# A mixer-and-experts block: second gate's weights behind the first expert's, routing on the residual's sums, first-layer weights laid out by partitions

## The chip, the cores and the metric

The kernel runs on one core of one Trainium2 chip. The metric is the device time of one execution in microseconds (us); the median of three runs is compared. All data are float32 in HBM, about 450 MB of it weights that are read once.

## What is computed

One block on 256 tokens of width 1024. A condition row `c` makes six modulation rows; a mixer (attention with forget gates, gated linear attention, pooling) works on the modulated x; the first layer norm follows; then 32 experts, 4 per token, and the second layer norm.

```python
cond = silu(c)
shift1, scale1, gate1, shift2, scale2, gate2 = split(cond @ w_ada + b_ada, 6)
h = x * (1 + scale1) + shift1
z = h @ w_in + b_in                      # 1024 -> 2582: heads, gates, pool inputs
y = concat([o_fox, o_gla, o_pool]) @ w_out
x = layer_norm(2**0.25 * x + (1 + gate1) * y, ln1_g, ln1_b)
h = x * (1 + scale2) + shift2
logits = h @ w_router + b_router         # 32 experts
gate = softmax(top_k(logits, 4))
y = sum over a token's 4 experts of gate * (clamped_swiglu(h @ w_gate_up[e] + b) @ w_down[e] + b)
x = layer_norm(2**0.25 * x + (1 + gate2) * y, ln2_g, ln2_b)
```

## The kernel before

**Loads.** All large weights pass through ring tiles of 2 MB (16 KB in each of 128 partitions), and SyncE issues their loads in the order of the program text. Each load waits until the slot that it gets is free, and the next one waits behind it. Ahead of the experts the ring has 5 slots (`NA`). In order they hold the first modulation's weights (`ada`) and the input projection's (`wz`), alternating; two small groups of constants; the rest of the input projection; the second modulation's shift and scale (`adam`); the output projection (`wo`); and the two gates' weights, `ada_g1` and `ada_g2` (`adag`, two tiles each). Then come the experts: four tiles of `w_gate_up` (`g`), with two tiles of `w_down` (`d`) of the expert before behind them. A second ring of 3 slots (`NB`, `ring2`) is opened for the experts; it lies on memory that the first layer's tiles (`early`) leave. Of every eight expert tiles, the first five go to the first ring and the last three to the second. The sum of the two is how far loads run ahead of TensorE.

**Layout.** `w_ada`, `w_in` and `w_out` are read from HBM as they are, with k rows by partitions: for `ada`, each piece read in one go is 128 columns (512 B) in the first tile and 256 columns (1 KB) in the others; for `wz`, 1520 and 272 columns; for the other tiles, 1024 or some 400.

**First layer.** `tokens_to_columns` transposes x on TensorE (4 transposes for each of four groups) and copies it to `hT`. `modulate` makes shift and scale of a pair of columns and applies them to `hT` in place. The k loop then multiplies `hT[:, k]` with the 1792 columns of `wz1[k]`: 6 products (`pqk`) and 8 (`pz`); a float32 product shows as two instructions in the trace. Attention, linear attention and pool follow and fill `oT`, the left operand of the output projection (`py`, 64 instructions; L134 is the line of the helper `mm` that issues nearly all products).

**Gates.** `ada_g1` and `ada_g2` are each summed on VectorE over k with weights `cond` (one multiply and seven multiply-adds, each over 1024 columns), to `acc` and `g2p`. Both stand in front of the output projection in the text. `last_scale` completes `g2p` behind expert 0's gate-up products, and `down` of each expert multiplies with it.

**Routing**, for each half t of the tokens: residual `y` in two column halves with `bn_stats`; norm to `n1`; 8 transposes of `n1`; scale `hA` and shift `hB` on the way out of PSUM to `h2T`; the router product in four groups of 32 rows, re-summed by a second product; top 4; positions `posm`. When both halves are done, `dispatch` of the first pair of experts makes one-hot rows `pp`, gathers `xg` from `n1` by products (`pxg`, 16 instructions for each half of the tokens), and scales it by `hA`, `hB`.

**Experts.** For each expert, `gate_up` (64 instructions and the bias), the clamp, the transposes, and one expert later `down`. Pairs share a dispatch. In front of expert 12 (`PAIR_MORE` = 6 pairs) all loads up to eight tiles ahead are issued, and then a branch on the largest expert's count is taken (`more_slots`; not entered with these inputs).

## Time and profile before

| | us |
|---|---|
| median of 3 runs | 1128.66 |
| lowest and highest | 1127.93, 1134.68 |
| profiled execution | 1129.8 |
| its span, first to last instruction | 1128.0 |
| TensorE matmul busy | 1035.4 (92%) |
| VectorE busy | 318.7 (28%) |
| ScalarE busy | 98.8 (9%) |
| mean DMA rate | 398 GB/s |

Matmul ends are modelled, so a busy TensorE is not one at its peak. The granted clock is given as a share of 2.4 GHz; 0.50 is 1.2 GHz. A queue's instruction (SPq) spans the time in which the listed issues were made, waits included.

### The profile page before, as it was taken

The page shows a single profiled execution, that of the slowest core. Times are in us where ns is not written, and L with a number is a line of the kernel's source. Part 1 is how long each engine was busy: PE and PEld are TensorE (multiplying, and loading weights), DVE is VectorE, ACT ScalarE, POOL GpSimd, SP SyncE. Part 2 cuts the span into 40 slices and gives each one's busy share as a digit, 9 for nine tenths or more (in the row PEclk, how much of TensorE's full clock was granted, in tenths as well). Part 3 has the DMA queues.
Part 4 walks back from the last instruction along what each step waited for, and adds up shares of the span by engine and source line. Part 5 has one row for each costly group of instructions (what it writes and reads, how often), then busy time and mean ns, then how long its engine had stood idle before and what let it go on. Part 6 is the DMA issues. An engine that isn't in the chain of part 4 may idle for free.

```text
span 1128.0 us, 11046 instructions
## 1 busy us (share of the span) xinstructions
PE 1035.4 (92%) x4734; PEld 436.9 (39%) x4735; DVE 318.7 (28%) x587; ACT 98.8 (9%) x205; POOL 41.5 (4%) x43
## 2 busy tenths in 40 slices
PE   6999998999999999996999999989989898989795
PEld 3656545434333333333344343423333333333231
DVE  1459694322222122211122221213221121211113
ACT  1024112100000000000000000000000000000100
POOL 2270000000000000000000000000000000000000
PEclk9999897999999999998999999999999999999998
DMA  9997499999999999999899999999999999999992
GB/s 324 348 385 283 181 378 373 428 423 428 428 428 427 428 428 428 428 427 423 344 427 428 428 428 426 428 427 428 428 428 427 428 429 427 428 427 428 428 414 92
DMA packets 52998, 449.49 MB, mean 398 GB/s; under 512 B 5056, under 2 KB 18768, under 8 KB 28496
## 3 DMA queue, kind: packets, MB, share of 16 engines
q1 hardware_dynamic: 52320, 447.90, 95.7%
q8 instruction: 39, 0.64, 0.2%
q10 hardware_dynamic: 624, 0.83, 0.2%
q14 instruction: 15, 0.12, 0.0%
HBM read 447.67 MB, written 1.05 MB: 398 GB/s over the span
## 4 chain that ended last, share of the span: by engine, by line
PE 29%; DMA 22%; DVE 1%; issue 1%; ACT 0%; POOL 0%; DVEq 0%; POOLq 0%
DMA d<-in_w_down 22%; PE gu L134 13%; PE py L134 7%; PE pxg L134 4%; PE ya L134 3%; PE pyl L134 1%; PE paT L837 1%; DVE yb L855 0%; DVE aT L839 0%; DVE res L919 0%; ACT n L931 0%; PE pln L134 0%; DVE r L1038 0%; DVE yl L1015 0%; DVE st L1019 0%
## 5 line engine op out<-in xcount | busy, mean ns | idle before, releaser
L134 PE MATMUL gu<-g,xg 128*64 128x512 f32 x2048 | 462.5, 595 | 14.0 <-DMA g<-in_w_gate_up 12.6
L134 PEld LDWEIGHTS gu<-g,xg 128*64 128x64 f32 x2048 | 143.2, 137 | 295.5 <-issue 261.0
L134 PE MATMUL py<-d,aT 128*64 128x512 f32 x992 | 227.1, 600 | 13.8 <-DMA d<-in_w_down 12.5
L825 DVE TENSOR_SCALAR g<-gu 128x512 f32<-128x512 f32 x32 | 22.1, 692 | 410.1 <-PE gu L134 410.1
L134 PEld LDWEIGHTS py<-d,aT 128*64 128x64 f32 x992 | 70.0, 137 | 150.5 <-issue 140.8
L134 PE MATMUL pxg<-pp,n 128*128 128x128 f32 x512 | 77.0, 302 | 14.9 <-DVE aT L839 7.0
L134 PEld LDWEIGHTS pxg<-pp,n 128*128 128x128 f32 x512 | 69.2, 208 | 43.0 <-issue 29.6
L855 DVE TENSOR_TENSOR yb<-py,g2p 64x512 f32<-64x512 f32 x60 | 41.3, 689 | 139.0 <-PE py L134 138.4
L134 PE MATMUL ya<-yb,sg_None 128*128 128x512 f32 x120 | 58.2, 607 | 4.9 <-DVE yb L855 4.8
L829 ACT ACTIVATE s<-g 128x512 f32<-128x512 f32 x32 | 20.2, 630 | 464.4 <-DVE g L825 464.4
L793 DVE TENSOR_SCALAR xg<-pxg,hA,hB 128x128 f32<-128x128 f32 x64 | 25.8, 409 | 99.2 <-PE pxg L134 90.0
L791 ACT ACTIVATE xg<-pxg,hB,hA 128x128 f32<-128x128 f32 x64 | 28.7, 457 | 274.3 <-DVE xg L793 273.6
L134 PE MATMUL pz<-wz,hT 128*128 128x512 f32 (+2 forms) x128 | 52.4, 547 | 0.0
L169 POOL TENSOR_TENSOR rsb<-rtb,half 128x2 f32<-128x2 f32 x1 | 0.7, 701 | 950.9 <-DVE rtb L168 950.9
L839 DVE COPY aT<-paT 128x512 f32<-128x512 f32 x32 | 22.1, 692 | 43.9 <-PE paT L837 43.8
L134 PE MATMUL py<-wo,oT 128*128 128x512 f32 x64 | 30.9, 629 | 0.2 <-ACT oT L642 0.2
L134 PEld LDWEIGHTS ya<-yb,sg_None 128*128 128x128 f32 x120 | 20.4, 189 | 26.9 <-issue 17.4
L134 PEld LDWEIGHTS pz<-wz,hT 128*128 128x128 f32 x128 | 23.4, 190 | 17.3 <-issue 14.3
L837 PEld LDWEIGHTS paT<-kc,l 128*128 128x128 f32 x128 | 18.0, 209 | 25.3 <-DVE l L831 15.4
L837 PE MATMUL paT<-kc,l 128*128 128x128 f32 x128 | 23.7, 308 | 0.0
L831 DVE TENSOR_TENSOR l<-l,s 128x512 f32<-128x512 f32 x32 | 22.1, 691 | 3.4 <-DVE l L830 0.5
L134 PE MATMUL pqk<-hT,wz 128*128 128x256 f32 x96 | 22.2, 381 | 0.7 <-DVE hT L332 0.7
(245 smaller groups left out, 519.1 us busy)
## 6 DMA issues: line engine op xcount, KB each, us to landing
g<-in_w_gate_up SPq DMA_DIRECT2D x128, 2048.0 KB, 30.4
d<-in_w_down SPq DMA_DIRECT2D x62, 2048.0 KB, 30.4
adam<-in_w_ada SPq DMA_DIRECT2D x4, 2048.0 KB, 16.7
adag<-in_w_ada SPq DMA_DIRECT2D x4, 2048.0 KB, 9.0
ada<-in_w_ada SPq DMA_DIRECT2D x6, 1024.0 KB, 11.1
wz<-in_w_in SPq DMA_DIRECT2D x8, 760.0 KB, 9.5
wo<-in_w_out SPq DMA_DIRECT2D x2, 1536.0 KB, 10.0
ada<-in_w_ada SPq DMA_DIRECT2D x4, 512.0 KB, 7.4
```

The source lines that it names most:

```text
L134: T.matmul(o, l, r, start=start, stop=stop, skip_group_check=True, **kw)
L169: G.tensor_tensor(o, t[:, :n], half[:, :n], op=OP.pow)
L791: A.activation(xg[:, k], bs[k // 4][:, k % 4], AF.Identity, bias=hB[:, k:k + 1], scale=hA[:, k:k + 1])
L793: V.tensor_scalar(xg[:, k], bs[k // 4][:, k % 4], hA[:, k:k + 1], hB[:, k:k + 1], op0=OP.mult, op1=OP.add)
L825: V.tensor_scalar(g, gu[:, 0], LIMIT, None, op0=OP.min)
L829: A.activation(s, g, AF.Sigmoid, scale=SW_ALPHA)
L831: V.tensor_mul(l, l, s)
L837: T.transpose(b[:, j], act[:, j::4], ident)
L839: V.tensor_copy(aT, b)
L855: V.tensor_mul(yb[m * CAP:(m + 1) * CAP, n * 512:(n + 1) * 512], b[r], g2p[r, n * 512:(n + 1) * 512])
```

## The change

- `w_ada`, `w_in` and `w_out` are laid out ahead of the kernel so that each ring tile is one contiguous run per partition (7 to 16 KB); each of `ada`, `wz` and `wo` is loaded by one DMA where it had two.
- x is given a second time, transposed (`xT`), and loaded straight into `hT`; `tokens_to_columns` goes. x itself is loaded behind `wo`.
- The first gate's weights are loaded ahead of `wo`, and summed ahead of the linear attention's output part; the router's weights are loaded earlier.
- The second gate's weights are loaded as two more tiles behind expert 0's four gate-up tiles, and summed behind expert 0's gate-up products; `last_scale` moves behind expert 1's. The place of the three second-ring tiles in each eight changes from the last three to the fourth to sixth.
- Routing: the router's weights are multiplied by `hA` and `hB` once (`wr2`, and their column sums `rrow`). The residual `y` is transposed as it is, before the norm; the logits are (product with `wr2`) times the norm's scale plus a row. The first pair's one-hot rows and gather are made for each half inside the loop, to `xgA`.
- Some tiles share memory to make room for `xgA` (`o_gla` with `z_gr`, the bias rows with `oT`, and others).

```diff
-            i = int(turn[0] % (NA + NB) >= NA)
+            i = int(3 <= turn[0] % (NA + NB) < 3 + NB)
...
+    def summed(acc, ts):
+        A.mul(acc, ts[0], cond[:, 0:1])
+        for k in range(1, KT):
+            V.scalar_tensor_tensor(acc, ts[k], cond[:, k:k + 1], acc, op0=OP.mult, op1=OP.add)
+    def load_columns(j, i, name):
+        t = ring_tile(name)
+        o = (4 + 2 * (3, 4, 2, 5).index(j) + i) * 4096
+        SY.dma_start(t, w_ada[:, o:o + 4096])
+        return [t[:, k * D:(k + 1) * D] for k in range(4)]
...
-            t = t.rearrange("p (k s n) -> p k s n", k=KT, s=2)
-            for h in range(2):
-                SY.dma_start(t[:, :, h], w_ada[0, :, h * D + cc * 256:h * D + (cc + 1) * 256]
-                             .rearrange("(k p) n -> p k n", p=P))
+            SY.dma_start(t, w_ada[:, cc * 4096:(cc + 1) * 4096])
...
-            SY.dma_start(t[:, 0:W1], w_in[0, k * P:(k + 1) * P, 0:W1])
-            SY.dma_start(t[:, W1:], w_in[0, k * P:(k + 1) * P, C_GA:])
+            SY.dma_start(wz1[-1][:, k % 2], w_in[:, k * WZ:(k + 1) * WZ])
...
-        SY.dma_start(xs[:, :, 0:256], xv[:, :, 0:256])
+        SY.dma_start(hT[:, 0:2], xTv[:, 0:2])
         load_z1(0)
-        SY.dma_start(xs[:, :, 256:], xv[:, :, 256:])
         first_ada[1]()
+        SY.dma_start(hT[:, 2:], xTv[:, 2:])
...
+        ada_g1 = load_cols(2, "adag1")
         wo = {}
...
-        ada_g1 = load_cols(2, "adag1")
-        ada_g2 = load_cols(5, "adag2")
+        SY.dma_start(xs, x[0].rearrange("(t p) d -> p t d", p=P))
...
-        tokens_to_columns(0, "z")
         modulate(0, 1)
...
+        acc1 = la_.tile([P, D], F32, tag="acc", name="acc1")
+        summed(acc1, ada_g1)
+        o_gla = la_.tile([P, TT, GVW], F32, tag="gr", name="o_gla")
...
+        for j, h in enumerate((hA, hB)):
+            V.tensor_mul(wr2[:, j], wr, h[:, :, None].to_broadcast([P, KT, NE]))
+        V.tensor_reduce(wrs, wr2.rearrange("p j k e -> p j e k"), axis=AX.X, op=OP.add)
+        mm(b[:, 0:2 * NE], ones, wrs.rearrange("p j e -> p (j e)"), True, False)
+        mm(b[:, NE:2 * NE], colv[:, 80:81].to_broadcast([P, P]), kc[:, K_I4:K_I4 + NE], False, True)
+        V.tensor_copy(rrow, b[:, 0:2 * NE].rearrange("p (j e) -> p j e", j=2))
...
                 V.bn_stats(st6[:, n], y)
+                b = bank(f"ph{t}{n}").rearrange("p (j s) -> p j s", j=4)
+                for j in range(4):
+                    T.transpose(b[:, j], twos(xs[:, t], 4 * n + j), ident)
+                A.copy(h2T[:, 4 * n:4 * n + 4, t * P:(t + 1) * P], b)
...
+            V.scalar_tensor_tensor(row, rrow[:, 0], nmr, rrow[:, 1], op0=OP.mult, op1=OP.add)
+            b = bank(f"plg{t}")
+            for k in range(KT):
+                mm(b[:, 0:NE], h2T[:, k, t * P:(t + 1) * P], wr2[:, 0, k], k == 0, k == KT - 1)
+            V.scalar_tensor_tensor(lg[:, t], b[:, 0:NE], rs, row, op0=OP.mult, op1=OP.add)
...
-            for k in range(KT):
-                g = slice(32 * (k // 2), 32 * (k // 2) + 32)
-                mm(b[g, :P], wr[:, k], h2T[:, k, t * P:(t + 1) * P], k % 2 == 0, k % 2 == 1)
-            V.tensor_scalar(lgp[:, t * P:(t + 1) * P], b[:, :P], colv[:, 80:81], None, op0=OP.add)
...
+            one_hot(ppA, posm[:, :, 0:2], t)
+            if t == 0:
+                first = [bank(f"pxgA{q}", "z").rearrange("p (j s) -> p j s", j=4) for q in range(2)]
+            gathered(first, ppA, t)
+        modulated(xgA, first)
...
         jobs += [("up", e, load_up, (e, i)) for i in range(4)] + (late or [])
+        if e == 0:
+            jobs += [("gate", 0, lambda e, i: load_columns(5, i, f"adag2_{i}"), (0, i)) for i in range(2)]
...
         if e == 0:
+            summed(g2p, weights("gate", 0))
+        elif e == 1:
             last_scale()
```

## Rows read from the trace of the kernel before

**Rows 1.** The page's slices: DMA rate in 40 equal slices of the span.
```profile
GB/s 324 348 385 283 181 378 373 428 423 428 428 428 427 428 428 428 428 427 423 344 427 428 428 428 426 428 427 428 428 428 427 428 429 427 428 427 428 428 414 92
```

**Rows 2.** Stretches: length, busy us (instructions) by engine, granted clock, DMA share, GB/s.
```profile
196.00:540.00 344.00, 323.76 (x1506) 127.95 (x1502) 73.92 (x135) 20.55 (x42) 0.00 (x0) 0.99 1.01 427
540.00:552.00 12.00, 10.93 (x54) 3.83 (x52) 3.03 (x7) 1.00 (x2) 0.00 (x0) 1.00 0.65 257
```

**Rows 3.** DMA issues: one expert tile's size, median us to landing.
```profile
g<-in_w_gate_up SPq DMA_DIRECT2D x128, 2048.0 KB, 30.4
```

**Rows 4.** Timeline of SyncE's queue, from separate windows: start, us, tile loaded, count.
```profile
107.87 32.63 SPq L214 DMA_DIRECT2D adag<-in_w_ada  x4
...
147.09 19.43 SPq L737 DMA_DIRECT2D g<-in_w_gate_up  x8
...
164.54 1.98 SPq L737 DMA_DIRECT2D g<-in_w_gate_up  x4
...
190.91 0.33 SPq L742 DMA_DIRECT2D d<-in_w_down  x1
```

**Rows 5.** Timeline: expert 0's first gate-up products on TensorE.
```profile
187.21 7.09 PE L134 MATMUL gu<-g,xg 128*64 128x512 f32 x32
```

**Rows 6.** Stretches in which the DMA engines stood still or sagged.
```profile
126.00:141.00 15.00, 14.97 (x75) 8.91 (x75) 9.47 (x15) 0.98 (x2) 2.66 (x2) 0.96 0.01 4
...
188.00:194.00 6.00, 6.00 (x30) 1.98 (x28) 0.86 (x4) 2.32 (x4) 0.00 (x0) 1.00 0.58 197
```

**Rows 7.** Stretches of the first layer, up to expert 0's first product.
```profile
2.00:22.00 20.00, 13.08 (x68) 7.18 (x68) 3.17 (x9) 2.85 (x6) 4.15 (x7) 1.00 1.09 343
24.20:71.00 46.80, 46.30 (x177) 29.98 (x173) 19.72 (x33) 6.30 (x12) 22.03 (x19) 1.00 1.04 355
71.00:121.40 50.40, 46.81 (x236) 31.67 (x236) 42.29 (x67) 19.80 (x48) 6.73 (x7) 0.99 0.89 333
121.40:164.50 43.10, 42.83 (x139) 20.48 (x139) 34.34 (x52) 2.04 (x5) 4.51 (x3) 0.93 0.62 241
...
164.50:187.20 22.70, 17.37 (x97) 13.51 (x96) 13.94 (x56) 7.41 (x16) 0.56 (x1) 0.70 1.01 416
```

**Rows 8.** Timeline of TensorE in the input projection.
```profile
24.23 2.46 PEld L134 LDWEIGHTS pqk<-hT,wz 128*128 128x128 f32 x12 [0.84 <-DMA wz<-in_w_in]
...
28.67 0.60 PE L338 MATMUL xT<-kc,n 128*128 128x128 f32 x4
...
67.36 3.60 PE L134 MATMUL pz<-wz,hT 128*128 128x512 f32 x8
```

**Rows 9.** Timeline of GpSimd and VectorE: bias rows, first write of `oT`, second gate's sum.
```profile
75.95 1.05 POOL L287 CAST bg<-bgf 32x1024 bf16<-32x1024 f32 x1
...
90.83 0.87 DVE L474 TENSOR_SCALAR oT<-pq,colv 128x256 f32<-128x256 f32 x2
...
151.36 6.56 DVE L624 SCALAR_TENSOR_TENSOR g2p<-adag,cond,g2p 128x1024 f32<-128x1024 f32 x5
```

**Rows 10.** Timeline of the routing of the second half, up to the first pair's gather.
```profile
165.17 1.22 PE L675 MATMUL ph<-kc,n 128*128 128x128 f32 x8 [0.67 <-ACT n L667]
165.36 0.69 DVE L662 SCALAR_TENSOR_TENSOR n<-n,yg 128x512 f32<-128x512 f32 x1
...
178.24 0.19 DVE L690 COPY lg<-plt 128x32 f32<-128x32 f32 x1 [0.73 <-PE plt L134]
...
181.59 5.69 PE L134 MATMUL pxg<-pp,n 128*128 128x128 f32 x32
...
186.38 0.41 DVE L793 TENSOR_SCALAR xg<-pxg,hA,hB 128x128 f32<-128x128 f32 x1 [2.98 <-PE pxg L134]
```

**Rows 11.** Timeline: nearest rows for the new copy and the new router product.
```profile
21.71 0.59 ACT L340 COPY hT<-xT 128x512 f32<-128x512 f32 x1
...
107.68 1.94 PE L134 MATMUL pcol<-kc,accm 128*128 128x4 f32 x16
```

**Rows 12.** Chain of waits: a later gather of 32 instructions at 2.4 GHz.
```profile
565.28 3.97 PE pxg L134 x32
```

183 lines of the change are left out of this document (84 added, 99 removed).

## The prediction

> **What bounds the kernel now.** I read the page's slices first. From the seventh slice on the DMA engines move some 428 GB/s almost without a break, and only the first six slices, one in the middle and the last lie lower [rows 1]. The stretches say the same: 427 GB/s from 196 to 540 us, a hole at 540 to 552 [rows 2]. So the expert weights are a stream, 32 x 6 tiles of 2048 KB, one tile in 2.10 MB / 428 GB/s = 4.9 us [rows 2, 3], and the end is the moment from which this stream runs unbroken, plus what is left to load then, plus the hole and the tail. The kernel is decided in its first 200 us.
>
> When does the stream become unbroken? SyncE's queue shows it [rows 4]: the loads of the first gate's and second gate's weights (adag, four tiles from 107.87) wait for ring slots, eight expert tiles go out from 147.09, and the ninth load, the first of expert 0's down weights, at 190.91. At that point the ring of eight is full and a slot comes free only when TensorE has used a tile: expert 0's products start at 187.21 [rows 5] and use one tile (16 of their instructions, half of 7.09 us) in 3.55 us, so 187.21 + 3.55 = 190.8. The DMA engines had already stood still from 126 to 141 us (4 GB/s), and sag once more around this point (197 GB/s from 188 to 194) [rows 6]; after it they are never short of slots until the hole at 540. The hole is the drain in front of the run-time branch after expert 11; it is the same number of tiles ahead in both kernels, so I move it along unchanged. The formula is therefore: end = (start of expert 0's products) + 3.55 + 4.9 x (tiles not yet issued) + a constant. Before: 190.9 + 184 x 4.9.
>
> **What the change moves in this formula.** Two terms, of opposite sign.
>
> *Tiles left.* Before, the second gate's two tiles are loaded in the idle time ahead of the experts. After, they take two of the eight slots that are filled ahead of expert 0's products; two of expert 1's tiles fall behind. 194 - 8 = 186 tiles remain in place of 184: **+9.8 us**. This is a cost at full price, as the stream they join has no free time [rows 2].
>
> *Start of expert 0's products.* Step by step along TensorE, which is the busy engine here (46.3 of 46.8 us, 46.8 of 50.4, 42.8 of 43.1 in the three stretches up to 164.5 [rows 7]).
>
> A, first layer's loads. TensorE starts the second k step at 24.23, released by a DMA [rows 8]; from there to 67.36 + 3.60 = 70.96 it has no wait. Up to there the loads ran at 343 GB/s [rows 7]; of the 22.2 us from 2.0 on I take off 1.7 for the way from last byte to release (an estimate; without it the gain is 4.4), so 20.5 us x 343 = 7.0 MB. Runs of 7 to 16 KB per partition are like those of the expert tiles, so I give these loads 428: 16.4 us, a gain of 4.1. Two of the four groups of x transposes (0.60 each [rows 8]) lie behind 24.23 and vanish: 1.2. Together **-5.2**; if the rate doesn't change, -1.2 is left. The row speaks against a rule here: at 343 GB/s runs of 512 B and 1 KB are far from the 427 that the long runs reach. The Trainium skill's "DMA: Bandwidth & Descriptors", section Specifications, puts the least transfer for line rate at 512 B; by that rule the old layout was at line rate already and the new one brings only the 1.2. That is the third rival below.
>
> B, from 71 to 121 TensorE and VectorE (42.3 of 50.4 us busy [rows 7]) both follow what came earlier; I carry A through unchanged: **0**. Earlier second-layer scale weights could let VectorE start its sums earlier and spare up to 3, somewhat under the 3.6 us in which TensorE isn't busy here; a worse order could cost one such step, 1.3 [rows 9].
>
> C, 121.4 to 164.5, the output projection, nearly all TensorE. The sum for the first gate is now placed ahead, in VectorE's free time (34.3 of 43.1 us busy [rows 7]), and its weights' two loads stand in SyncE's queue before the projection's: those wait for slots that came free at 107.87 (the first adag load [rows 4]) and shortly after, so less A they land about ten us before 121.4. The loads of the second gate go, and their sum with them, five of its seven steps being the 6.56 us of VectorE just ahead of the first projection result [rows 9]; TensorE is the later one there, so this gains nothing. New is that the transposes and the router product of the first 128 tokens can be queued inside the projection: 8 transposes, 1.22 us [rows 10], and 16 products with 128-column stationary loads, nearest row 1.94 us [rows 11]. I take both on the path: **+3.2** (0 if they stay behind).
>
> D, from the residual of the second half to its logits: before, 165.36 + 0.69 = 166.05 to 178.24 [rows 10], 12.2 us (norm, scale, transposes behind the first half's routing, scale and shift, grouped product, re-sum). After: four transposes 0.6, ACT copy 0.59 [rows 11], half to all of the 1.94, hops 0.3, so 2.5 to 3.4; the statistics run beside it on VectorE and GpSimd. The gather of the first half (1.98, half of [rows 12]) can stand in between, TensorE's queue being in order; 4.0 to 5.9 then. I take 4.0: **-8.2** (-9.5 to -6.3).
>
> E, logits to gather, 178.24 to 181.59, is unchanged: **0**. F, the gather: before 32 instructions, 5.69 us, mostly at the lower of the two clocks (1.2 GHz; the stretch has 0.70 granted on average [rows 7, 10]); the first half's 16 go ahead, and the last 16 take 2.0 at 2.4 GHz [rows 12] or 2.85 at 1.2. With the first scaled column block (0.41 [rows 10]) no longer covered in full: **-2.8** (-3.7 to -2.6).
>
> Clock: before, it was back at 2.4 GHz when expert 0 began, after the long gather. With a shorter gather the first tile may run at 1.2 GHz: 0 to +1.8; I take **0**, as the first half's gather comes closer.
>
> Sum: -5.2 + 3.2 - 8.2 - 2.8 = **-13.0**: products start at 174.2, the ring resumes at 177.8. End: 177.8 + 186 x 4.9 against 190.9 + 184 x 4.9: **-3.3 us**. The terms at their good ends give -21.4, at their bad ends -8.1, so -11.6 to +1.7 at the end (with the 1.3 of B and the 1.8 of the clock in it).
>
> What goes at nothing: x loaded a second time (1 MB, 2.4 us of DMA) sits behind the projection's weights, where the engines stand idle anyway; without that idle time it would be 2.4. The second gate's sum, now one ACT multiply and seven VectorE steps of some 1.3 us [rows 9], lies under the products of experts 0 and 1; its result is wanted at expert 0's down product, two times 14 us later, and each step can hold expert 0's clamp by at most 1.3, paid by TensorE, which has slack against the stream. The bias rows, split by GpSimd up to 77.0, now lie where the mixer's output is first written at 90.83 [rows 9]; both move together. The product for the last scale moves from expert 0 to expert 1, past nothing that waits. The router's folded weights are five short VectorE steps and three small products ahead of the first gate's row, in VectorE's free time.
>
> **Rivals.** (1) *The whole gain arrives*: the two extra tiles are hidden and -13 stands, 1115.7. It needs free time in the stream behind expert 0, which [rows 2] deny up to 540. (2) *The loads come late, slower than before.* Three of the first eight tiles lie in the second ring, on memory of the first layer. Those places must be freed by the mixer's last readers. In the trace of before the three follow the last projection product within 2 us [rows 4], and nothing shows that they could go sooner, since the queue stood before them. If they are held until 164.5 - 5.2 + 3.2 = 162.5, five tiles (24.5 us) have still to come and the ring is full only at 187: the stream, not TensorE, sets the time, 162.5 + 191 x 4.9 = 1098.4 against 1092.5, **+5.9**, 1134.6. It decides once these loads go later than 177.8 - 24.5 = 153. Against it: the last readers of that memory (the mixer's inputs, scores and gate) run ahead of the transposes that feed the projection's last 24 of 64 instructions. (3) *The layout does not do what it says*: A is -1.2, -9 + 9.8 = +0.8, 1129.5.
>
> **Numbers.** The sum stands against the profiled execution, 1129.8 with a span of 1128.0; the median, 1128.66, lies 1.1 lower. -3.3 on the median is 1125.4; I say **1125**. Chances: forecast 0.65 (1117 to 1130), rival 1 0.08, rival 2 0.12, rival 3 0.10, others 0.05. One per cent, 11.3 us, is about what a measurement of this kernel tells from no change. Faster by more: rival 1 and the good end of the forecast, 0.11; slower by more: 0.03; within: 0.86. The range **1117 to 1134** leaves out rival 1, the far half of rival 2 and the others, just under 0.2.
>
> **What would show it.** The second k step starts near 20; the last projection product ends near 162; the first expert product near 174, right behind a gather of 16; a pause of the DMA engines of some 8 us before that with the ring full; the next load 3.6 us after the first expert product; all that follows shifted by 3 us, with the same hole and tail. Wrong would be: no pause (rival 2), a second k step at 24 (rival 3), or the end shifted as much as expert 0's start (rival 1).

## The result and the profile after

The changed kernel takes 1135.81 us (median of 10 runs, 1134.28 to 1139.32); the kernel before, on the same chip, 1128.3 (10 runs, 1126.05 to 1134.68). The ratio is 1.0056 with a 95% interval of 1.0036 to 1.0077: **slower by 0.6%**, less than the one per cent taken as no change, but on the other side of zero from the forecast of 1125 and above its range, which ended at 1134. The profiled execution took 1137.03 with a span of 1135.3, so 7.3 more than the span of before; the two traces show the difference that the medians show (7.5). The ten executions of the changed kernel lie in two groups, five at 1134.3 to 1134.7 and five at 1136.9 to 1139.3, and the profiled one is of the second.

The page's slices answer to [rows 1]:

```profile
GB/s 364 376 336 259 286 370 170 430 428 427 428 428 427 428 427 426 429 427 425 354 430 427 429 426 427 427 429 427 427 429 426 429 428 425 428 428 427 427 418 114
```

The stream from the eighth slice on and the dip in front of the branch are the same. The first six slices differ, and the seventh now has a real hole, 170 in place of 373. The stretches answer to [rows 2, 6, 7] (start:end, length, busy us of PE, PEld, DVE, ACT and POOL with their instructions, granted clock, DMA share, GB/s):

```profile
2.00:22.00 20.00, 13.57 (x63) 7.60 (x64) 2.39 (x8) 2.53 (x5) 4.11 (x7) 1.00 0.98 391
24.20:71.00 46.80, 45.97 (x172) 28.24 (x171) 19.28 (x34) 6.26 (x11) 24.96 (x21) 1.00 1.02 395
71.00:121.40 50.40, 47.19 (x210) 31.03 (x210) 40.95 (x65) 20.42 (x48) 3.39 (x4) 0.90 0.70 281
113.00:120.00 7.00, 6.53 (x30) 4.51 (x28) 5.25 (x7) 3.10 (x6) 0.00 (x0) 0.53 1.03 442
121.40:164.50 43.10, 41.70 (x162) 23.49 (x162) 21.93 (x40) 2.46 (x6) 2.04 (x2) 0.96 0.83 328
164.50:187.20 22.70, 18.60 (x102) 14.20 (x102) 17.18 (x64) 7.65 (x15) 1.11 (x2) 0.80 0.40 151
178.00:189.00 11.00, 8.41 (x31) 5.67 (x33) 8.81 (x29) 3.11 (x7) 0.00 (x0) 0.53 0.05 14
196.00:540.00 344.00, 318.51 (x1480) 124.91 (x1478) 73.68 (x135) 21.37 (x43) 0.00 (x0) 1.00 1.01 427
```

Two things stand out. The DMA engines pause from 178 to 189 (14 GB/s): the eight slots are full and the stream waits for TensorE, as forecast. (The long pause of before, 126 to 141, is filled by expert tiles: 328 GB/s from 121.4 to 164.5 in place of 241, and 151 behind it in place of 416.) And TensorE's granted clock is 0.53, close to 1.2 GHz, in two places, 113 to 120 and 178 to 189, with TensorE's gaps in front of both (shown below); a shorter such stretch, between 71 and 80, comes up in the last part. SyncE's queue answers to [rows 4] (start, us, tile loaded, count; separate windows):

```profile
85.31 9.97 SPq L236 DMA_DIRECT2D adag<-in_w_ada  x2
108.82 3.53 SPq L322 DMA_DIRECT2D wo<-in_w_out  x2
...
121.43 20.46 SPq L772 DMA_DIRECT2D g<-in_w_gate_up  x4
146.33 0.81 SPq L236 DMA_DIRECT2D adag<-in_w_ada  x2
...
190.76 3.76 SPq L772 DMA_DIRECT2D g<-in_w_gate_up  x2
```

The first gate's loads now go ahead of the projection's, and the second ring's three, the fourth gate-up tile and the second gate's two, have gone by 147. The last row is the load on which the prediction's formula rests: **190.76 us, where it was 190.91**. The start of the stream has hardly moved, and it has two more tiles to carry. TensorE, from the input projection to expert 0, answers to [rows 5, 8, 10] (start, us, line, operation, tiles, shape, count, and in brackets idle time and what ended it):

```profile
11.40 4.35 PE L162 MATMUL pqk<-hT,wz 128*128 128x256 f32 x12 [0.70 <-DVE hT L380]
...
22.62 2.86 PE L162 MATMUL pqk<-hT,wz 128*128 128x256 f32 x12
...
66.19 3.60 PE L162 MATMUL pz<-wz,hT 128*128 128x512 f32 x8
...
72.39 12.88 PE L162 MATMUL pz<-wz,hT 128*128 128x406 f32 x32
...
108.63 1.94 PE L162 MATMUL pcol<-kc,accm 128*128 128x4 f32 x16
...
112.31 0.86 PE L162 MATMUL po<-pT,z 128*64 128x256 f32 x4 [1.36 <-ACT pT L594]
...
121.49 0.86 PE L162 MATMUL po<-pT,z 128*64 128x256 f32 x4
...
167.89 2.82 PE L162 MATMUL py<-wo,oT 128*128 128x512 f32 x6
...
178.87 0.64 PE L162 MATMUL ppos<-msel,kc 128*128 128x32 f32 x2 [1.70 <-DVE msel L727]
...
180.27 3.79 PE L162 MATMUL pxgA<-g2p,n 128*128 128x128 f32 x16
185.64 8.51 PE L162 MATMUL gu<-g,xgA 128*64 128x512 f32 x32 [1.58 <-ACT xgA L222]
```

The first of these rows and the last attention product (`po`) have these counterparts in before:

```profile
12.91 2.86 PE L134 MATMUL pqk<-hT,wz 128*128 128x256 f32 x12 [0.70 <-DVE hT L332]
...
117.78 0.86 PE L134 MATMUL po<-pT,z 128*64 128x256 f32 x4
```

From all these rows and their counterparts the difference is made up as follows (us, after minus before):

| step | forecast | measured | from |
|---|---|---|---|
| A: end of the input projection | -5.2 | -1.2 | 69.79 against 70.96 |
| B: from there to the last attention product | 0 | +4.9 | end 122.35 against 118.64 |
| C: from there to the end of the output projection | +3.2 | +2.45 | 48.35 against 45.9 |
| D: last residual to its logits | -8.2 | -7.3 | 4.93 against 12.2 |
| E: logits to gather | 0 | -0.2 | 3.17 against 3.35 |
| F: gather to expert 0's first product | -2.8 | -0.25 | 5.37 against 5.62 |
| start of expert 0's products | -13.0 | -1.6 | 185.64 against 187.21 |
| expert 0's first products | 0 | +1.4 | 8.51 against 7.09 |
| next load | -13.0 | -0.15 | 190.76 against 190.91 |
| two more tiles, at 626 us | +9.8 | +9.65 | the same load at 636.38 against 626.71 |
| from there to the end | 0 | -2.2 | rest of +7.3 |

### The profile page after: what moved, and what is told of

The parts are those of the page before. It is cut to its first block, busy times and chain, and to the rows that moved or that the text cites. A ratio compares the mean times of both kernels' runs of the same rounds, so it can differ in the third digit from the quotient of the medians.

```text
span 1135.3 us, 11005 instructions
## 1 busy us (share of the span) xinstructions
PE 1037.6 (91%) x4718; PEld 438.9 (39%) x4719; DVE 313.0 (28%) x581; ACT 98.5 (9%) x201; POOL 39.4 (3%) x43
## 4 chain that ended last, share of the span: by engine, by line
PE 28%; DMA 23%; DVE 1%; issue 0%; ACT 0%; POOL 0%; DVEq 0%; SPq 0%; POOLq 0%
DMA d<-in_w_down 21%; PE gu L162 12%; PE py L162 7%; PE ya L162 3%; PE pxg L162 3%; DMA g<-in_w_gate_up 1%; PE pyl L162 1%; PE paT L872 1%; DVE yb L890 0%; DVE aT L874 0%; DVE res L954 0%; ACT n L966 0%; PE pln L162 0%; PE pl L162 0%; DVE yl L1052 0%
## 5 line engine op out<-in xcount | busy, mean ns | idle before, releaser
L162 PE MATMUL gu<-g,xg 128*64 128x512 f32 x1024 | 233.0, 598 | 11.2 <-DMA g<-in_w_gate_up 11.1
L162 PE MATMUL gu<-g,xgA 128*64 128x512 f32 x1024 | 233.0, 598 | 10.0 <-DMA g<-in_w_gate_up 6.2
L162 PEld LDWEIGHTS gu<-g,xgA 128*64 128x64 f32 x1024 | 72.5, 137 | 151.2 <-issue 132.7
L162 PEld LDWEIGHTS gu<-g,xg 128*64 128x64 f32 x1024 | 71.2, 137 | 153.4 <-issue 132.4
L162 PE MATMUL pxg<-pp,n 128*128 128x128 f32 x480 | 69.8, 294 | 11.9 <-DVE aT L874 7.1
L162 PEld LDWEIGHTS pxg<-pp,n 128*128 128x128 f32 x480 | 62.5, 201 | 39.2 <-issue 25.7
L224 DVE TENSOR_SCALAR xg<-pxg,hA,hB 128x128 f32<-128x128 f32 x32 | 12.9, 409 | 45.0 <-PE pxg L162 40.1
L222 ACT ACTIVATE xg<-pxg,hB,hA 128x128 f32<-128x128 f32 x32 | 14.4, 457 | 122.9 <-DVE xg L224 122.6
L222 ACT ACTIVATE xgA<-pxg,hB,hA 128x128 f32<-128x128 f32 x28 | 12.6, 457 | 143.1 <-DVE xgA L224 142.9
```

Of the source, the lines that this page charges most:

```text
L162: T.matmul(o, l, r, start=start, stop=stop, skip_group_check=True, **kw)
L222: A.activation(xg[:, k], bs[k // 4][:, k % 4], AF.Identity, bias=hB[:, k:k + 1], scale=hA[:, k:k + 1])
L224: V.tensor_scalar(xg[:, k], bs[k // 4][:, k % 4], hA[:, k:k + 1], hB[:, k:k + 1], op0=OP.mult, op1=OP.add)
```

## The experiments

Each was timed in five rounds (one in three) beside the kernel before, whose median was 1128.4 to 1129.4 on each chip; ratios are to that. "After" is the changed kernel, 1135.81.

**The second gate back in front of the experts (e1).** Its two tiles are loaded behind the first gate's and the projection's, and summed ahead of the projection's results. The ring's second part moves by two places and the one-hot rows get memory of their own, both for that reason alone.

```diff
+        ada_g2 = load_cols(5, "adag2")
...
+        summed(g2p, ada_g2)
...
-            jobs += [("gate", 0, lambda e, i: load_columns(5, i, f"adag2_{i}"), (0, i)) for i in range(2)]
-            summed(g2p, weights("gate", 0))
```

> The changed kernel, with one part undone: the second gate's two tiles are loaded and summed ahead of the output projection again (and the second ring takes the second to fourth expert tile, so that no early expert load waits for the projection's weights). Theory 1, two tiles added to a stream without free time cost 9.8 us: the load that waits for the first expert product has 184 tiles behind it in place of 186, so about 1126 against 1135.8 for the changed kernel, 2 below the kernel before. The start of expert 0's products may move by a few us either way, and the end with it. Theory 2, the loss sits in the stages ahead of the experts and the two tiles were free: 1133 to 1137, as the changed kernel.

Measured: 1125.91 (1124.44 to 1129.17), ratio 0.9975 [0.9955, 0.9994]; 9.9 below after. The start of the stream is the same:

```profile
190.69 3.76 SPq L779 DMA_DIRECT2D d<-in_w_down  x2
```

190.69 against 190.76, and 9.9 us less: the two tiles cost their full price, 9.8 by the forecast. This term of the formula is shown.

**The second gate's sum later (e2).** The order in which an engine issues its instructions isn't that of the text, and in after this sum begins between the last steps of the routing: its first multiply (184.09) is just in front of ScalarE's copy of the first gathered columns (185.15).

```profile
110.60 1.15 ACT L228 ACTIVATE acc<-adag,cond 128x1024 f32<-128x1024 f32 x1 [4.15 <-PE pcol L162]
111.78 0.48 ACT L594 COPY pT<-ppT 128x384 f32<-128x384 f32 x1
...
184.09 1.15 ACT L228 ACTIVATE g2p<-adag,cond 128x1024 f32<-128x1024 f32 x1 [0.80 <-PE pxgA L162]
185.15 0.79 ACT L222 ACTIVATE xgA<-pxgA,hB,hA 128x128 f32<-128x128 f32 x2
```

These are ScalarE's rows in after: two pairs of the same kind, one of each gate's sum. In e2 the sum's weights are made to depend on expert 0's activation.

```diff
+            cl = one.tile([P, KT], F32, tag="cl", name="cl")
+            V.scalar_tensor_tensor(cl, act[:, 0:KT], 0.0, cond, op0=OP.mult, op1=OP.add)
-            summed(g2p, weights("gate", 0))
+            summed(g2p, weights("gate", 0), cl)
```

> The changed kernel, with the second gate's sum made to depend on expert 0's activation, so that none of its steps can be queued between the copies that scale the first gathered columns. Theory 1, the sum in front of those copies ate the gain of the shorter gather: expert 0's products start 1.5 to 3 us sooner than the 185.6 of the changed kernel, their first 32 instructions take 7.1 us in place of 8.5, and the time falls by 2 to 4, to 1132 to 1134. Theory 2, the gather and the first tile are slow for their clock alone (1.2 GHz from 178 to 189): start within 0.5 us, time 1135 to 1136.

Measured: 1136.96 (1134.7 to 1138.02), 1.0061 [1.004, 1.0082]: no gain. The trace shows what came of it (TensorE, SyncE's queue, VectorE):

```profile
184.69 7.09 PE L162 MATMUL gu<-g,xgA 128*64 128x512 f32 x32 [1.34 <-ACT xgA L222]
...
195.69 3.76 SPq L777 DMA_DIRECT2D d<-in_w_down  x2
...
208.58 6.53 SPq L772 DMA_DIRECT2D g<-in_w_gate_up  x4
...
204.60 9.20 DVE L230 SCALAR_TENSOR_TENSOR g2p<-adag,cl,g2p 128x1024 f32<-128x1024 f32 x7
```

Expert 0 starts 0.95 sooner, its first products take 7.09 in place of 8.51, and the first down load goes 2.4 sooner (195.69 against 198.06). But the gate's two ring slots come free only when VectorE has read them, now from 204.60 on, and the next expert load waits for that until 208.58 where it went at 198.96. That costs the stream about half of the gain: the DMA engines move 383 to 410 GB/s from 205 to 220 where they moved 423 to 429 in after, 1.2 us of stream. The loads are still 1.1 ahead of after at 520 us (522.37 against 523.48) and lose that behind it, where two executions of one kernel differ by as much (see the last part). The sum's place is bound on both sides: before expert 0 it stands in the way of the routing, behind it it holds two slots of eight.

**The first gate's sum later (e3).** The same device, with the sum's weights made to depend on the last attention output.

```diff
+        c1 = la_.tile([P, KT], F32, name="c1")
+        V.scalar_tensor_tensor(c1, oT[:, 2, 0:KT], 0.0, cond, op0=OP.mult, op1=OP.add)
-        summed(acc1, ada_g1)
+        summed(acc1, ada_g1, c1)
```

> The changed kernel, with the first gate's sum made to depend on the last attention output, so that none of its steps stands between the copies of the attention scores. Theory 1, those steps cost the stretch from 71 to 122 us some 3 of the 4.9 us that it lost: the last attention product ends near 119.5 in place of 122.35, the output projection follows, and the time falls by about 3, to 1133. Theory 2, the stretch is late because its input is late and its clock is low (the second part of the input projection ran at 1.2 GHz): last attention product at 122, time 1135 to 1137.

Measured: 1136.92 (1136.2 to 1138.1), 1.0063 [1.0038, 1.0087]. Two stretches of it:

```profile
113.00:120.00 7.00, 5.75 (x37) 3.70 (x36) 5.86 (x8) 2.61 (x6) 0.00 (x0) 1.00 1.00 428
126.00:135.00 9.00, 8.12 (x30) 5.96 (x29) 4.42 (x8) 1.39 (x2) 0.00 (x0) 0.50 0.16 67
```

With the multiply out of the way TensorE keeps 2.4 GHz in 113 to 120 (0.53 in after), and from the first column sums to the last attention product it takes 10.96 us, as before the change, in place of 13.72. But that is not the multiply alone. The same stretch in e2, which has the multiply in front as after does and the same wait of 1.36, and in e6 (below), which has no multiply there and a wait of 0.57:

```profile
113.00:120.00 7.00, 5.79 (x37) 3.80 (x36) 6.91 (x8) 4.00 (x7) 0.00 (x0) 1.00 0.99 421
```

```profile
113.00:120.00 7.00, 6.50 (x29) 4.25 (x27) 4.96 (x7) 2.46 (x5) 0.00 (x0) 0.52 1.02 417
```

In e2, and in e5, the clock stays at 1.00 and the way to the last attention product takes 11.76; in e6 the clock falls and it takes 12.94. So of B's +4.9 the hoisted multiply costs 0.8, and 2.0 are a stretch at 1.2 GHz that can come with it or without it; what brings it isn't shown.

Besides, in e3 VectorE does the sum between the steps of the linear attention; TensorE waits there (0.89 at 127.77), the clock is 0.50 from 126 to 135, the first projection product comes at 134.38 (129.23 in after), and expert 0 starts at 187.03. The gain is given back within 15 us.

**The layout, taken back and alone (e4, e12).** e4 is after with the old layout of the weights and x transposed on TensorE; e12 is before with the new layout. Each is the layout's part of the change's diff, so only its first lines stand here.

```diff
-            SY.dma_start(t, w_ada[:, cc * 4096:(cc + 1) * 4096])
+            for h in range(2):
+                SY.dma_start(t[:, :, h], w_ada[0, :, h * D + cc * 256:h * D + (cc + 1) * 256]
+                             .rearrange("(k p) n -> p k n", p=P))
```

> The changed kernel, with its layout undone: the three weights are read with k rows by partitions in pieces of 512 B to 6 KB, x is loaded once at the start and transposed on TensorE; the order of the loads and the routing stay as changed. Theory 1, the layout brings the 1.2 us that the end of the input projection moved: about 1137. Theory 2, it brought the 5 us that were forecast, and something later gave them back (the order of the gate's loads and sum): 1140 to 1141. Theory 3, the layout itself is what made the stretch from 71 to 122 us late: 1131 to 1133.

> The kernel before with the layout alone: the three weights by partitions, x also by columns and the transposes gone, x itself behind the projection's weights; routing, gates and order of the loads as before. Theory 1, it is worth what the end of the input projection moved, 1.2, to 1.7: 1126.5 to 1127.5. Theory 2, it is worth the 5.2 that were forecast, and only the changed order of the gates hid it: 1123 to 1124. Theory 3, its earlier tiles make the scheduled order of the later steps worse and it costs: 1129 or more.

Measured: e4 1137.54 (1137.07 to 1140.26), 1.0066 [1.0041, 1.009], 1.7 above after. e12 1127.08 (1125.79 to 1134.64), 0.9989 [0.9968, 1.001], 1.9 below the kernel before on that chip. Both medians speak for the layout, by 1.7 and 1.9 where 5.2 was forecast, but neither is clear of noise (e12's interval reaches over 1), and the third pair of kernels that differ in the layout alone comes out the other way: e6 1127.74 without it, e10 1129.16 with it. Nor do the traces show a gain that reaches the stream: in e12 the load that waits for expert 0's first products goes at 191.42 (190.91 in before), and the load of 513.99 in before goes at 513.94; its span is 2.4 shorter by what happens behind that. That the layout is worth anything at the end is not shown.

**The second k step's weights first (e5).** In after the loads go at 391 GB/s up to 22 us, and the second k step still starts only at 22.62, because 2 MB of modulation weights stand in front of its own.

```diff
-        load_ada1(1)
         load_z1(1)
+        load_ada1(1)
```

> The changed kernel, with one pair of loads exchanged: the second k step's weights of the input projection (0.9 MB) stand ahead of the second tile of modulation weights (2 MB), which that step does not use. Theory 1, the start of the second k step is set by the bytes in front of its weights: it falls from 22.6 to about 18, the input projection ends up to 3 us sooner than 69.8, and the time falls by 2 to 3, to 1133. Theory 2, TensorE has work or the later tiles bind (2 MB of modulation weights are only shifted behind): the projection ends at 69 to 70 and the time stays at 1135 to 1136.

Measured: 1135.63 (1133.98 to 1137.61), 1.007 [1.0049, 1.0091]: no gain in the median. The second step starts at 21.30, but the third has to wait for its modulation:

```profile
30.15 1.05 PE L162 MATMUL pm<-kc,part 128*128 128x4 f32 x8 [0.79 <-ACT part L366]
...
31.90 4.54 PE L162 MATMUL pqk<-hT,wz 128*128 128x256 f32 x12 [0.70 <-DVE hT L380]
```

The projection's first part ends at 71.8 in place of 69.8. TensorE had used part of the wait for the second step's weights: 4 of the 16 instructions of the next modulation's products stand in it in after and 12 behind the second step's first products, and in e5 all 16 come behind the second step. Still, in this trace the next load goes at 187.57, 3.2 sooner than in after, and the span is 1132.4, 2.9 shorter. That isn't the exchange, which cost 2.0 up to there: this execution has a granted clock of 1.00 where after's fell (71 to 80, and 113 to 120).

**Routing alone (e6).** Before, with the routing part of the change and nothing else.

```diff
+            V.scalar_tensor_tensor(row, rrow[:, 0], nmr, rrow[:, 1], op0=OP.mult, op1=OP.add)
+            V.scalar_tensor_tensor(lg[:, t], b[:, 0:NE], rs, row, op0=OP.mult, op1=OP.add)
...
+            gathered(first, ppA, t)
```

> The kernel before with the routing part of the change alone: the router product on the residual's sums, the gather of the first pair ahead and the columns kept in their own memory; the layout, the order of the loads, the gates' loads and sums stay as before. Theory 1, the routing's gain arrives: residual to logits 5 us in place of 12.2, the output projection 2.5 longer, the tail 2.3 shorter (the last part of the changed kernel's trace), the next load at about 186 in place of 190.9: 1121 to 1122. Theory 2, it arrives only in part, since the loads wait for the projection's weights and the DMA engines had only some 3 us of idle time in front of 190.9: 1123 to 1125. Theory 3, it is eaten up again by TensorE's lower clock in the gather and the first tile: 1126 to 1128.

Measured: 1127.74 (1123.75 to 1131.83), 0.9985 [0.9964, 1.0005]. Expert 0 starts at 180.42 and the next load goes at 184.43, 6.5 sooner than before, yet the end comes only 3.7 sooner in the traces and the medians differ by 1.1. The same stretch in e6 and in before:

```profile
165.00:195.00 30.00, 27.48 (x142) 15.33 (x140) 12.96 (x54) 5.65 (x12) 0.57 (x1) 0.89 1.00 412
```

```profile
165.00:195.00 30.00, 25.17 (x135) 16.24 (x137) 14.98 (x60) 9.54 (x20) 0.56 (x1) 0.77 0.93 375
```

In before the DMA engines moved 375 GB/s here; at 412 they are busy all the time. Without the earlier second-ring loads, only (412 - 375) x 30 = 1.1 MB, 2.6 us of stream, could be won: a sooner start helps as far as the ring was full before it.

**Neither gate moved (e10).** Layout and routing, with both gates' loads, sums and the ring as before: what would be left of the change without the gates.

```diff
-        ada_g1 = load_cols(2, "adag1")
         wo = {}
...
+        ada_g1 = load_cols(2, "adag1")
+        ada_g2 = load_cols(5, "adag2")
...
-            i = int(3 <= turn[0] % (NA + NB) < 3 + NB)
+            i = int(turn[0] % (NA + NB) >= NA)
```

> The change without its two gate moves: layout and routing as changed; order of the loads, both gates' sums and the split of the rings as before. Theory 1 (the stream decides): expert 0's products start at 178 to 180, but its ring is filled no sooner than about 186, since the loads wait for the projection's weights, so that the time is 1124 to 1126, 10 below the changed kernel and little below the kernel before. Theory 2, the start decides as in the forecast's formula: 190.9 falls to 182, and with the 2.3 of the tail the time is 1118 to 1119. Theory 3, the layout costs what the routing brings: 1128.

Measured: 1129.16 (1127.13 to 1132.28), 1.0001 [0.9982, 1.0021]. The number is nearest to theory 3's, but the reason is none of the three. VectorE's rows:

```profile
158.55 0.69 DVE L705 TENSOR_TENSOR yg<-py,g1p 128x512 f32<-128x512 f32 x1 [0.51 <-PE py L162]
159.16 1.28 DVE L668 SCALAR_TENSOR_TENSOR g2p<-adag,cond,g2p 128x1024 f32<-128x1024 f32 x1
160.35 0.68 DVE L706 SCALAR_TENSOR_TENSOR n<-n,yg 128x512 f32<-128x512 f32 x1
160.95 1.28 DVE L668 SCALAR_TENSOR_TENSOR g2p<-adag,cond,g2p 128x1024 f32<-128x1024 f32 x1
```

The second gate's sum runs into the first half's residual, a 1.28 step between each two of its steps. TensorE later waits 3.98 for the first half's selection (at 172.93), and expert 0 starts at 189.33, 9 us behind e6, where the sum ends at 157, ahead of the residual. That the sum's place is all of these 9 us was not tested.

**Two unused products where TensorE waits (e7, and again as e16).** e1 with two products whose result nobody reads, tied to the second half's logits, in front of the positions. They keep TensorE busy in the wait just ahead of the stretch of 178 to 189.

```diff
+            if t:
+                b = bank("fill")
+                for j in range(2):
+                    mm(b[0:NE], lg[:, t], n1[:, 0, 0:512], True, True)
```

> The second gate's weights early, as in the first experiment (1125.9), and two products whose result nobody uses (32 x 512, about 1 us each) on TensorE in the idle time behind the second half's logits. Theory 1, what the short gather lost it lost to the clock, which falls in that idle time: with the engine busy there the last 16 instructions of the gather take 2.0 us in place of 3.8, the first 32 of expert 0's products 7.1 in place of 8.7, the next load goes out at 187 in place of 190.7, and the time is 1122. Theory 2, the clock does not follow that idle time, or the copies of the gathered columns bind: 1125 to 1126; the two products can also cost their own time, then 1127.

> The seventh kernel again, for a comparison on one chip: 1124 to 1125, 0.996 of the kernel before.

Measured: 1124.59 (1122.92 to 1127.23), 0.9963 [0.9947, 0.998], and again 1123.98 (1122.6 to 1126.32), 0.9946 [0.9929, 0.9964]. In e7's trace (TensorE, then a stretch):

```profile
175.80 1.90 PE L162 MATMUL fill<-n,lg 128*32 128x512 f32 x4 [0.34 <-DVE lg L718]
...
179.19 2.15 PE L162 MATMUL pxgA<-ppA,n 128*128 128x128 f32 x16 [0.26 <-DVE ppA L210]
182.66 7.09 PE L162 MATMUL gu<-g,xgA 128*64 128x512 f32 x32 [1.31 <-ACT xgA L222]
...
165.00:195.00 30.00, 27.39 (x149) 14.89 (x150) 14.99 (x59) 7.75 (x14) 0.80 (x2) 1.00 0.82 331
```

The clock stays at 1.00; the gather of 16 takes 2.15 (3.79 in after), expert 0's first 32 instructions 7.09 (8.51), and the next load goes at 186.35, 4.3 before e1's, although 1.9 us of work were added. For the gather the fillers are shown to hold the clock: its 16 instructions take 2.12 to 2.15 in all six kernels that have them and 3.31 to 3.79 in the ten with the new routing that don't. For the first tile they are not: seven of those ten take 7.09 as well, and only e1 and after over 8. And 1.7 of the 4.3 were there ahead of the fillers, since the second half's logits are read at 175.49 here and at 177.15 in e1. So 2.7 lie behind the logits (in e16 too), 1.1 of them up to expert 0's first product and 1.6 in its first tile. The two traces of this kernel differ in one thing near the end (e7, then e16):

```profile
1063.00:1069.00 6.00, 5.33 (x18) 1.46 (x16) 0.00 (x0) 1.17 (x2) 0.00 (x0) 0.72 1.00 426
```

```profile
1063.00:1069.00 6.00, 5.27 (x23) 1.91 (x22) 1.34 (x2) 1.16 (x2) 0.00 (x0) 1.00 0.99 421
```

With the clock's fall (0.72) the span is 1123.0, without it 1121.2. e1 has no fall there either, and against it e16's next load comes 3.8 sooner (186.87) and its end 3.7: in the traces the formula's other term, the start of the ring, holds one for one too. The medians, from different chips, are 1.3 (e7) and 1.9 (e16) below e1's, and the intervals of the ratios overlap, so that the gain in time is less sure than the gain in the trace.

**Fillers in the tail (e15).** e7 with three more unused products, 128 x 512, behind the gate-up products of experts 28, 29 and 30.

```diff
+        if e in (28, 29, 30):
+            b = mps.tile([P, 512], F32, tag="m", name=f"fill{e}")
+            for j in range(3):
+                mm(b, ident, kc[:, 0:512], True, True)
```

> The seventh kernel with three more products that nobody uses (128 x 512) behind the gate-up products of experts 28, 29 and 30, in TensorE's short waits for loads. Theory 1, the last 35 us are TensorE's, not the stream's, and a stretch at 1.2 GHz just ahead of them costs 1.7: with the waits filled the clock stays at 2.4 GHz and the time is 1123, 1.5 below the seventh kernel. Theory 2, the fillers stand in front of the products that the loads have just released and cost what they save: 1124 to 1126. Theory 3, the end follows the stream alone: 1124.5, as the seventh.

Measured: 1124.17 (1122.57 to 1125.75), 0.994 [0.9919, 0.996], span 1123.9. The granted clock still fell between 1063 and 1069 (0.72), and the medians of e15 and e16 are 0.2 apart. The last of these fillers ends at 1043, though, and TensorE's three waits of 0.67 just ahead of the fall (1062 to 1065) are left as they were; e16 has the same three waits and no fall. So work in the waits for loads did not hold the clock there; work in these three waits wasn't tried.

**The mixer's repairs together (e8), the first gate's multiply on GpSimd (e14).** e8 is e7 with the edits of e3 and e5. e14 is e7 with only the first multiply of the first gate's sum moved from ScalarE to GpSimd.

```diff
+            e.tensor_scalar(acc, ts[0], cond[:, 0:1], None, op0=OP.mult)
...
-        summed(acc1, ada_g1)
+        summed(acc1, ada_g1, G)
```

> The second gate's weights early, the two filling products, the second k step's weights ahead, and the first gate's sum behind the last attention output, all in one kernel. If the gains of the single parts add up (2 to 3 from the exchanged loads, 3.7 from the clock), the next load goes out at 184 to 185 and the time is 1119 to 1120, below both kernels. If every gain ahead of 120 us is given back by the clock behind it, as with the late sum alone, it is that of the filling products, about 1122.

> The seventh kernel (1124.6) with the first multiply of the first gate's sum on GpSimd in place of ScalarE, so that it no longer stands in front of the copies of the attention scores; every other instruction in the same order. Theory 1, that multiply is what opens TensorE's hole at 110 to 112: the hole shrinks from 1.4 to 0.6, the clock doesn't fall behind it, the last attention product ends at 119 to 120 in place of 122.4, and 2 to 3 us of it reach the end: 1122 to 1123. Theory 2, the clock falls anyway in the next hole (linear attention, 122 to 127) and takes it back, as in the third run: 1124 to 1125.

Measured: e8 1127.09 (1125.05 to 1129.22), 0.9992 [0.9979, 1.0005], no better than e7 alone: its clock is 0.50 from 126 to 137 and the next load goes at 191.99, as the parts had already shown one by one. e14 1125.53 (1124.52 to 1127.98), 0.9965 [0.9948, 0.9982], no better than e7. Its rows (GpSimd, VectorE):

```profile
111.54 3.93 POOL L231 TENSOR_SCALAR acc<-adag,cond 128x1024 f32<-128x1024 f32 x1 [5.62 <-PE pcol L162]
...
115.50 1.28 DVE L233 SCALAR_TENSOR_TENSOR acc<-adag,cond,acc 128x1024 f32<-128x1024 f32 x1 [2.67 <-POOL acc L231]
```

The last attention product starts at 120.42 (121.49 in after), but VectorE stands 2.67 us for the multiply, the next column sums wait 1.35 for VectorE, and the clock falls there: the next load goes at 188.86, 2.5 behind e7. Of that 1.4 lies ahead of the multiply, since the first column sums start at 109.50 (108.08 in e7) with a granted clock of 0.81 from 71 to 80 (1.00 in e7). Against e16 the next load comes 2.0 later and the end (span 1123.2) 2.0 later: one for one once more.

**The projection's weights first (e9, again as e13; e11).** e9 and e13 are after with the first gate's loads behind the projection's, and with the ring's second part moved by two places as in e1; e11 is e7 with both gates' loads behind the projection's.

```diff
-        ada_g1 = load_cols(2, "adag1")
         wo = {}
...
+        ada_g1 = load_cols(2, "adag1")
```

> The changed kernel, with the order of one pair of loads as before: the output projection's two tiles ahead of the first gate's two (and the second ring takes the second to fourth tile behind the routing). The second gate stays behind the first expert, 186 tiles. Theory 1, the projection's products are what TensorE does while the linear attention waits for other engines; with its weights landing at 116 to 121 instead of some 100, TensorE stood still there and fell to the lower clock. With the old order the first projection product comes at 121 to 124 in place of 129.2, the first gate's sum goes behind the attention by itself, expert 0's products start 3 to 5 us sooner than 185.6, and the time is 1131 to 1133. Theory 2, the order of these loads doesn't matter, the hoisted second sum and the clock behind the logits do: start 185 to 186, 1135 to 1136.

> The ninth kernel once more, for a trace of a usual execution. Theory 1 as there: 1131 to 1132, and its trace shows expert 0's products starting 3 to 4 us sooner than 185.6, with TensorE's idle time from 109 to 128 us at 1.8 in place of 3.0 and less time at 1.2 GHz behind it. Theory 2: the median of the ninth run was chance, 1135 to 1136 and a start at 185 to 186.

> Layout and routing as changed, both gates ahead of the experts with the projection's weights loaded first, the second ring for the second to fourth expert tile, and the two filling products behind the logits. If the order of the loads brings what the ninth run looks for and the filling products what they brought in the seventh, expert 0's products start at 178 to 179 in place of 182.7, the next load goes out near 182 with the ring full, and the time is 1120 to 1122. If the ring is not full by then (its last tiles wait for the projection's weights, free at about 165), it is 1124, as in the seventh run.

Measured: e9 1131.88 (1131.15 to 1136.07), 1.0022 [1.0002, 1.0041]; e13 1133.36 (1131.0 to 1137.17), 1.0033 [1.0015, 1.0052]. So 2.4 to 3.9 below after. Where it comes from stays open: in both, the profiled execution was the longest of its kernel, and in those traces expert 0 starts no sooner than in after (185.98 and 186.43). e11 missed what it was meant for: 1128.93 (1126.91 to 1130.37), 0.9985 [0.9965, 1.0005], some 4 above e7. Like e10 it has the wait of 3.98 us for the first half's selection, at 172.75, and its next load goes at 193.27.

The best version is thus e7 with its repetition: 4.2 to 5.4 us below the kernel before, some 11 below after (e15, with three more unused products, is no different).

## Why the prediction was wrong

**The formula was right.** Both of its terms were shown separately: two tiles for 9.9 (e1 against after), and, in the traces, the ring's start one for one (e16 against e1, e14 against e16, and nearly so e5 against after, 2.9 for 3.2). It holds where the ring is full by then, as the prediction had it and as after shows; in e6 it was not, and 6.5 brought 3.7. The range was lost in the second term.

**The step that failed is the sum for the start of expert 0's products**, "-5.2 + 3.2 - 8.2 - 2.8 = -13.0: products start at 174.2". They start at 185.64. Its terms:

- *A, -5.2, was mis-sized*: -1.2 in the trace, and that is its good end: in the twelve other traces with the same first loads the first part of the projection ends at 69.85 to 71.41, against 70.96 in before and 71.00 in e6. "I give these loads 428" failed: long runs moved 391 GB/s up to 22 us and 395 from 24 to 71, where the old layout had 343 and 355 [rows 7], and the expert stream 427. The old pieces of 512 B and 1 KB were indeed slower, so the rule of the Trainium skill ("DMA: Bandwidth & Descriptors", Specifications: at least 512 B for line rate) does not describe these rows in full; but its rival was the nearest to A's size. The other half of the loss is on TensorE. With the transposes gone the first k step starts 1.5 sooner (11.40 against 12.91), but its first 12 instructions take 1.5 longer (4.35 against 2.86, and 4.35 to 5.49 in those twelve traces): the first six take 661 ns each where before's take 396, though the granted clock reads 1.00 in both. The second k step came 1.6 sooner, but 12 instructions of modulation products now stood behind its first products, and e5 shows that putting its weights first only moves the wait to the third step. (The 1.7 us taken off for the way from last byte to release stands on no row; without it A would have been -5.6.)
- *B, "I carry A through unchanged: 0", with -3 and +1.3 as bounds, was wrong*: +4.9, in two parts. The first, 2.1, lies between the end of the projection's first part and the first column sums (38.84 against 36.73). 1.7 of it is TensorE's clock: the 32 instructions that take 12.88 from 72.39 on take 11.19 in e3, and 11.19 in before as well; the granted clock from 71 to 80 is 0.81 in after and 1.00 in the other two.

```profile
73.99 11.19 PE L162 MATMUL pz<-wz,hT 128*128 128x406 f32 x32
```

  1.0 comes with the new routing (37.77 in e6 against 36.73 in before, both at 1.00). One row bears on it: ScalarE's load of the exponential's table (1.28) lay in idle time at 89.78 in before, and stands at 95.86 behind the wait for `mx` in after, ahead of the first exponentials; TensorE then waits 0.78 for ScalarE's `eb` (at 99.84), which it doesn't in before:

```profile
95.86 1.28 ACT L522 ACT_TABLE_LOAD   x1 [6.16 <-DVE mx L519]
```

  It stands so in the kernels with the new routing (e3, e4, e6, e10 and others) and not in e12; that it is the reason wasn't tried by itself. The new layout takes 0.6 off (37.15 in e3 against 37.77 in e6, both at 1.00). The second part, 2.75, lies between there and the last attention product. 0.8 of it is the first gate's sum, which I had put at nothing "in VectorE's free time": its first step is a multiply on ScalarE, and it is issued at 110.60, in front of the copy that TensorE waits for (1.36 in place of 0.57). The other 2.0 is the stretch at 0.53 behind that wait, which e2 and e5 don't have with the same wait, and e6 has without the multiply.
- *C (+2.45 for +3.2), D (-7.3 for -8.2) and E* were right in mechanism and size. (D's own parts, 2.5 to 3.4 and 1.98, add up to 4.5 to 5.4 and not to "4.0 to 5.9"; 4.93 was measured. The bad ends add up to -7.8 and not -8.1. Neither decides anything.)
- *F, -2.8, came to -0.25, and the "0 to +1.8" for the clock to +1.4*: the short gather does run, but TensorE has waited 1.70 for the positions just before, and the gather and the first tile run at 1.2 GHz (0.53 from 178 to 189). The 2.85 "at 1.2" was too low a price: it is half of a row in which the clock changed (0.50 from 172 to 185 in before, 1.00 from 186 to 188), and 16 instructions at 1.2 GHz take 3.79. I had counted on "the first half's gather" coming closer to hold the clock; it ended at 174.68, and the work behind it has gaps. The fillers show the cause for the gather's 1.6; the first tile's 1.4 is the clock too, but it also goes without fillers, as in e2 and e3. To a lesser part it is the second gate's multiply in front of `xgA`, up to 0.95 by e2.

Added up, the next load misses the forecast by 12.9 us, and 6.7 of that is work at 1.2 GHz (1.7 and 2.0 in B, 1.6 in F, 1.4 in the first tile), for which the prediction had 0 to +1.8; 4.0 is A. Kernels with the same work at these places have some of the slow stretches and not others, one trace each, so that part of the 6.7 may belong to the execution that was traced and not to the change. What brings each of them, apart from the gather's, stays open.

**"All that follows shifted ... with the same hole and tail" held for the hole and not quite behind it**: of +9.65 at 626 us, +7.3 are left at the end. 0.8 goes between 626 and 651 us (the way between these two loads takes 24.6 in before and 23.9 in after), 0.3 up to the last expert load, and 1.35 behind that (32.5 and 31.2 to the end). Two executions of one kernel differ there by more: 25.6 and 23.4, 32.3 and 30.9 in e7 and e16. So no part of the change is needed to explain it.

**The rivals.** The first (the tiles are hidden) is refuted by e1. The second (second-ring loads late) did not occur: those loads had gone by 147, before 153, and the engines paused as forecast. It had the right sign for a reason that was not the right one. The third (layout) was near for A, and would have given 1129.5. None had the sums of the gates in it: I followed them as loads and as VectorE's time, and not as instructions in the order of ScalarE, or as readers that hold ring slots (e2). The range missed for the same reason, since B was bounded by one VectorE step, and because the lower clock was priced at 1.8 at most.

## What to carry to other kernels

A tile put into a saturated stream costs its full time, while the same tile loaded in the idle time ahead of it costs nothing; count this first, and then ask up to which load the ring was really full before crediting a sooner start. Work "in free time" has to be followed instruction by instruction on each engine that it touches, in the order in which the engine issues, up to the slot that its last read frees. And a wait of 1 to 2 us on TensorE in a chain of small steps can cost as much again in a slower stretch behind it, so a gain ahead of such a wait is easily given back; a few unused products in the wait ahead of the gather kept it at the higher clock in all six kernels that had them. But such stretches also came and went here between kernels with the same work: read the granted clock of every stretch, and compare more than two traces, before a difference of 2 us is credited to an edit.

## What the hardware did unexpectedly

- A 40.5 KB load (`colv`, ScalarE's queue) took 5.3 us to land behind the large first loads, where it took 2.2 before the change (DMA issues: tile, queue, count, size, median us):

```profile
colv<-in_cols ACTq DMA_DIRECT2D x1, 40.5 KB, 5.3
```

- Contiguous runs of 7 to 16 KB per partition moved 391 to 395 GB/s in the first 71 us and 427 in the expert stream of the same kernel.
- The same multiply of 128 x 1024 float32 by a column took 3.93 us on GpSimd (e14) and 1.15 on ScalarE.
- TensorE's first products of the input projection took 661 ns each in after and 396 in before, where they start 1.5 us later, at a granted clock of 1.00 in both.
- Between 71 and 80 us the granted clock is 0.81 in after, e2 and e14 and 1.00 in e3, e5 and e7, though after, e2, e3, e7 and e14 run the same instructions in the same order on each engine up to there; the same 32 instructions take 12.88 and 11.19 (after and e3).
- The clock near the end fell in one execution of a kernel and not in another (e7 and e16, 1063 to 1069), with spans 1.8 us apart; products added more than 20 us ahead of it did not prevent it (e15).
